# Moving one tap of a short convolution to ScalarE and GpSimd, and the z gate's two scalings to other steps

## The chip, the cores and the metric

One NeuronCore of a Trainium2 chip runs the whole program. The metric is the time of one execution in microseconds (us) of device time. A profile is one execution taken by the hardware profiler. PE is TensorE (PEld its weight loads), DVE is VectorE, ACT is ScalarE, POOL is GpSimd, SP is the engine whose queue issues most DMAs.

## The reference, cut to what matters

A decoder trunk of two layers on 512 tokens with model width 1024, in float32. Each layer normalizes its input, projects it with one wide matrix, and feeds three mixers: A (a gated MLP over positions), B (attention with a window of 128) and C (a gated delta rule). Their results are projected, weighted by sigmoid gates, summed and added to the input; a SwiGLU block follows. The change touches mixer C alone, in two places.

```python
def causal_short_conv(x, w):              # x: q, k and v of mixer C, 1536 channels
    xp = jnp.pad(x, ((0, 0), (DN_CONV - 1, 0), (0, 0)))
    out = xp[:, 0:S_] * w[0]
    for i in range(1, DN_CONV):           # DN_CONV = 4 taps
        out = out + xp[:, i:i + S_] * w[i]
    return jax.nn.silu(out)
...
    o = rmsnorm(o, norm_g) * jax.nn.silu(z)   # o: 4 heads x 128; norm_g: 128 weights, one per head channel
```

So each of the 1536 channels gets a causal filter of four taps, and the result of the delta rule is normalized, weighted by `norm_g` and gated by z.

## The kernel before, in words

Every float32 product of the projections is made of three matmuls: a weight tile is split into a high part `wh` (ACT) and a low part `wl` (DVE), the activations likewise, and high by high, high by low and low by high are summed in one PSUM bank. A projection tile of 128 x 1024 weights is 24 matmuls of 512 columns. Tiles that the convolution needs come out with channels on partitions (`fm_tile`, line 343); those of z come out with tokens on partitions (`tm_group`, line 349), four banks at a time. Four PSUM banks (`mm`) serve these projections, four (`px`) everything small.

The first half of a layer is called the mixing part here. One dense stream runs the projections in the order k, z, q and v of heads 0 and 1, q and v of heads 2 and 3, aq, gv, u (`ORDER`, line 44), and then the gates. Beside it run small streams: `decay` (line 583), `keys` (602), `queries` (640), `values` (665) and `scan` (678) of the delta rule, `blocks` (824) and `solves` (747) for its triangular systems, attention and the position mixing. `keys` sends a matrix to DRAM by a DMA on POOL's queue (`blkscr`), `blocks` fetches it back (`nx`), inverts 16 x 16 blocks on DVE and passes the result through DRAM again (`cols`), and `solves` begins with the products of `Tc`. The gates may not begin before the last step of `scan`, so what the dense stream has left by then (above all `u`, four tiles) is what PE has to fill the waits of the small streams with.

The order of PE's instructions is fixed when the program is built. A planner (`Issue`, lines 51 to 161) walks through all streams with costs of its own: an elementwise step on DVE or ACT counts 0.07 us plus columns / 960, a two-input step on POOL 0.1 us plus columns / 430, each with a latency `LAT` of 0.7 us on top. A small stream goes on at the time that the planner gives for its inputs; until then the dense stream fills in. Only PE's order is written out; the other engines' instructions are put in order by the framework, each engine's in one queue, and each engine works through its queue in order.

The convolution of one tile of 128 channels (`dn_conv`, line 530) takes the projection out of its bank with a scaling (`pre`, DVE), multiplies by the last tap on ACT (`cv`), adds the three other taps with one DVE instruction each, makes the SiLU with a tanh on ACT and a last DVE instruction that writes `dk`, `dq` or `dv`. `rot` buffers (five of them, line 190) hold `pre` and `cv`. There are 12 tiles per layer, 24 in all.

The z gate (`z_proj`, line 1104) is made per 128 tokens: a tanh on ACT out of the bank, a DVE instruction that forms (tanh + 1) times the bank's value, and a second DVE instruction that scales by the token's norm (`rsth`) and by the weight `dn` (`norm_g`, loaded repeated over all partitions, 128 x 128). That is four groups per layer, eight in all. `scan` later multiplies this gate with its normalized result, in place (`zg`). `branch_c` (line 1059) turns the result with PE transposes and splits it into a high part (`bH`, ACT) and a low part (`bL`, DVE) for the branch's projection.

A constant `pad` of `PAD` columns (line 224) stands among the first tiles and takes up room only.

Of the kernel before, what the change touches and what calls it, by code (L numbers as in the profile page):

```python
# [10 lines left out]
F32 = mybir.dt.float32  # L11
F32R = mybir.dt.float32r
I32 = mybir.dt.int32
AF = mybir.ActivationFunctionType
ALU = mybir.AluOpType
# [3 lines left out]
P = 128  # L19
T = 512  # L20
# [17 lines left out]
LAT = 0.7  # L38
DMA_LAT = 2.5
DENSE = 10  # L40
PAD = 112
SOON = 200
ORDER = "k z qv0 qv1 aq gv u"

# [120 lines left out]
def hybrid_kernel(ctx, tc, x0, pos, wi, wkv, wb, wo, wg, wd, gn, convw, lngb, sguw, sgub,  # L165
                  sinks, alog, dtb, dnn, wt, gf, out, depth=DEPTH):
    issue = Issue()
    nc = issue.front(tc.nc)
# [11 lines left out]
    def nm(s):  # L180
        uid[0] += 1
        return f"{s}_{uid[0]}"
# [7 lines left out]
    def rot(name):  # L190
        return base.tile([P, T], F32, tag="rot", name=nm(name), bufs=N_ROT)
# [7 lines left out]
    def cst(shape, name, dt=F32):  # L199
        return const.tile(shape, dt, name=name, tag=name)  # L200
# [22 lines left out]
    gnt = cst([P, 2 * DEPTH, KT], "gnt")  # L223
    cst([P, PAD], "pad")
    nc.sync.dma_start(gnt, gn)
# [207 lines left out]
    def layer(l, norm, first=None):  # L433
# [6 lines left out]
        def lp(shape, name, src, pool=lay):  # L440
            t = pool.tile(shape, F32, tag=name, name=nm(name))
            nc.sync.dma_start(t, src)
            return t

        cw = lp([P, 12, 4], "cw", convw[l])
        snk = lp([P, 8], "snk", sinks[l])
        al = lp([P, 4], "al", alog[l])
        db = lp([P, 4], "db", dtb[l])
        dn = lp([P, P], "dn", dnn[l])
        lnc = lp([P, 8], "lnc", lngb[l])  # L450
        nsnk = lay.tile([P, 8], F32, tag="nsnk", name=nm("nsnk"))
        nc.vector.tensor_scalar(nsnk, snk, -1.0, None, ALU.mult)
# [1 line left out]
        def br_tiles(th, tl):  # L454
            return ([pg(th, "brH", dt=F32R) for i in range(4)], [pg(tl, "brL", dt=F32R) for i in range(4)])
# [5 lines left out]
        banks = yield from tm_group(first or [wkv[l, j] for j in range(4)], 264, xs, ("mm", "px", "px", "px"))  # L461
        vt = pg("kv", "vt", [P, NCH, P])
        rst8 = lay.tile([P, NCH], F32, tag="rst8", name=nm("rst8"))
        rsth = lay.tile([P, NCH], F32, tag="rsth", name=nm("rsth"))
# [65 lines left out]
        def dn_conv(ti, dst, ps):  # L530

            yield f"rep{norm.gi}"
            pre = rot("pre")
            nc.vector.tensor_tensor(pre, ps, norm.rep, ALU.mult)
            cv = rot("cv")
            nc.scalar.activation(cv, pre, AF.Copy, scale=cw[:, ti, 3:4])
            for i in (2, 1, 0):
                n = 3 - i
                nc.vector.scalar_tensor_tensor(cv[:, n:], pre[:, :T - n], cw[:, ti, i:i + 1], cv[:, n:],
                                               ALU.mult, ALU.add)  # L540
            nc.scalar.activation(pre, cv, AF.Tanh, scale=0.5)
            nc.vector.scalar_tensor_tensor(dst, pre, 1.0, cv, ALU.add, ALU.mult)
# [14 lines left out]
        def hs(hl):  # L557
            return slice(hl * P, (hl + 1) * P)
# [500 lines left out]
        def branch_c():  # L1059

            for e in (f"gA{l}", f"A{l}", f"o{l}0{NCH - 1}", f"o{l}1{NCH - 1}"):
                yield e
            bH, bL = br["C"] = br_tiles("fm", "kd")
            for i in range(4):
                pt = bank("px")
                for c in range(NCH):
                    nc.tensor.transpose(pt[:, hs(c)], zg[c][:, hs(i)], ident)
                nc.scalar.copy(bH[i], pt)
                nc.vector.tensor_tensor(bL[i], pt, bH[i].bitcast(F32), ALU.subtract)
                yield  # L1070
            issue.set(f"C{l}")

# [31 lines left out]
        def z_proj():  # L1104
            banks = yield from tm_group([wi[l, CI_Z + j] for j in range(4)], 512, xs)
            yield f"gg{l}"
            for c in range(NCH):
                z = zg[c]
                nc.scalar.activation(z, banks[c], AF.Tanh, scale=rsth[:, c:c + 1])
                nc.vector.scalar_tensor_tensor(z, z, 1.0, banks[c], ALU.add, ALU.mult)  # L1110
                zv = z.rearrange("p (h e) -> p h e", h=4)
                nc.vector.scalar_tensor_tensor(zv, zv, rsth[:, c:c + 1], dn.unsqueeze(1).broadcast_to([P, 4, P]),
                                               ALU.mult, ALU.mult)
            issue.set(f"z{l}")

        def keys_done():
# [17 lines left out]
        zg = [pg("zg", "zg", [P, T]) for c in range(NCH)]  # L1134
# [76 lines left out]
        with tc.tile_pool(name=f"ffn{l}", bufs=1, reuse_waits="tile") as fp:  # L1211
# [25 lines left out]
            for m in range(KT):  # L1237
                pd = mm_bank()
                for j, (k0, k1) in enumerate(((0, 8), (8, 16), (16, 22))):
                    w = wload(wd[l, m, :, k0 * P:k1 * P], (k1 - k0) * P)  # L1240
# [108 lines left out]
def _rep(a):  # L1349
    return np.ascontiguousarray(np.broadcast_to(a[..., None, :], a.shape[:-1] + (P,) + a.shape[-1:]))  # L1350


def _layout(x, positions, attn_norm, w_in, sgu_ln_g, sgu_ln_b, sgu_w, sgu_b, attn_sinks, dn_conv_w, dn_a_log,
            dn_dt_bias, dn_norm, w_branch, w_out, ffn_norm, w_gate_up, w_down, final_norm):
    L = w_in.shape[0]
    cuts = np.cumsum([0, 512, 512, 512, 128, 128, 1536, 512, 4, 4, 3072])
    perm = np.concatenate([np.arange(h * 64, (h + 1) * 64) for h in HEAD_PERM])
    wi, wkv, wb, wg, wd, wo = [], [], [], [], [], []
    for l in range(L):
        u, v, q, k, vb, qkv, z, be, a, gt = [w_in[l][:, cuts[i]:cuts[i + 1]] for i in range(10)]  # L1360
        wi.append(np.concatenate([_tiles_fm(qkv), _tiles_fm(u), _tiles_tm(q[:, perm]), _tiles_tm(v), _tiles_tm(z),
                                  _tiles_fm(gt)]))
        wkv.append(_tiles_tm(np.concatenate([k, vb, be, a], axis=1)))
        br = []
        for i in range(3):
            w = w_branch[l, i][perm] if i == 1 else w_branch[l, i]
            t = _tiles_fm(w)
            br.append(t.reshape(4, 2, P, 512).transpose(0, 2, 1, 3).reshape(4, P, 1024))
        wb.append(np.stack(br))
        wo.append(_tiles_fm(w_out[l]))  # L1370
        g = _tiles_fm(w_gate_up[l])
        wg.append(np.stack([g[:KF], g[KF:]], axis=1).reshape(2 * KF, P, 1024))
        if l < L - 1:
            wd.append(_tiles_fm(w_down[l]))
    gn = np.stack([attn_norm, ffn_norm], axis=1).reshape(2 * L, D)
    return {
        "x0": x[0].T.reshape(KT, P, T),
        "pos": positions[0].reshape(NCH, P).T,
        "wi": np.stack(wi), "wkv": np.stack(wkv), "wb": np.stack(wb), "wo": np.stack(wo), "wg": np.stack(wg),
        "wd": np.stack(wd),  # L1380
        "gn": gn.reshape(2 * L, KT, P).transpose(2, 0, 1),
        "convw": dn_conv_w.reshape(L, 4, 12, P).transpose(0, 3, 2, 1),
        "lngb": np.concatenate([sgu_ln_g, sgu_ln_b], axis=1).reshape(L, 8, P).transpose(0, 2, 1),
        "sguw": sgu_w.transpose(0, 3, 1, 2),
        "sgub": _rep(sgu_b.reshape(L, 512)).reshape(L, P, 4, P),
        "sinks": _rep(attn_sinks[:, HEAD_PERM]),
        "wt": w_down[L - 1].reshape(KF, P, D), "gf": _rep(final_norm),
        "alog": _rep(dn_a_log), "dtb": _rep(dn_dt_bias), "dnn": _rep(dn_norm),
    }


# [21 lines left out]
```

## Time and profile before

| what | value |
|---|---|
| three runs | 1724.6, 1725.21 (median), 1727.14 us |
| the profiled execution's own time | 1728.58 us |
| its span, first to last instruction | 1726.5 us |
| PE busy | 1706.7 us (99%) |
| DVE busy | 852.8 us (49%) |
| ACT busy | 648.0 us (38%) |
| POOL busy | 414.8 us (24%) |

The profiled execution took 3.37 us more than the median of the runs, and 2.08 us of its time lie outside the span. Matmuls overlap one another and their ends are modelled, so PE's busy share says where PE had work, not how fast it went; the waits in front of PE's instructions are what tells of lost time. The two mixing parts lie at about 9 to 315 us and 862 to 1172 us of the span; between and after them run the dense SwiGLU blocks.

### The profile page before, as it was taken

How to read it: one execution, taken by the hardware profiler on the slowest of the kernel's cores; microseconds unless marked ns; L12 is line 12 of the kernel's file. 1: busy time of each engine (PE TensorE's matmuls, PEld its weight loads, DVE VectorE, ACT ScalarE, POOL GpSimd, SP SyncE). 2: the span in 40 equal slices, each digit the busy share in tenths (PEclk: the TensorE clock that was granted, in tenths of full speed). 3: DMA queues.
4: the chain of work that ended last, by engine and by line, in shares of the span. 5: the costliest groups of instructions: out<-in, count | busy, mean ns of one | idle time of the engine just before them, and what ended most of it. 6: DMA issues, size and time to landing. Idle time of an engine off the chain costs nothing.

```text
span 1726.5 us, 22439 instructions
## 1 busy us (share of the span) xinstructions
PE 1706.7 (99%) x8580; PEld 1410.4 (82%) x8580; DVE 852.8 (49%) x1624; ACT 648.0 (38%) x1206; POOL 414.8 (24%) x457
## 2 busy tenths in 40 slices
PE   9999999999999999999999999999999999999998
PEld 8888778888888888888888877788888888888886
DVE  7685874544543333323276948644444433333224
ACT  6454663323342222222245546532233322222212
POOL 3423231021223333310024133210212233333000
PEclk9999999999999999999999999999999999999999
DMA  5232112232443223344332220122224534444332
GB/s 163 93 104 90 38 46 96 86 98 90 130 153 99 97 97 98 98 128 125 109 117 98 95 80 26 57 91 91 98 98 134 164 105 120 120 122 158 98 98 85
DMA packets 73116, 176.59 MB, mean 102 GB/s; under 512 B 24945, under 2 KB 25201, under 8 KB 73009
## 3 DMA queue, kind: packets, MB, share of 16 engines
q1 hardware_dynamic: 71184, 170.71, 31.0%
q0 software_dynamic: 1248, 3.41, 0.7%
q8 instruction: 67, 1.10, 0.3%
q10 hardware_dynamic: 576, 1.05, 0.2%
q14 instruction: 41, 0.33, 0.1%
HBM read 162.03 MB, written 13.11 MB: 101 GB/s over the span
## 4 chain that ended last, share of the span: by engine, by line
PE 95%; DVE 2%; ACT 1%; POOL 1%; issue 0%; DMA 0%; SPq 0%; POOLq 0%; ACTq 0%; DVEq 0%
PE mm L120 83%; PE px L120 12%; DVE U L120 0%; DVE wl L120 0%; DMA x<-in_x 0%; ACT pr L120 0%; POOL of L120 0%; DVE xf L120 0%; DVE pr L120 0%; DVE S L120 0%; DVE zg L120 0%; DVE Tc L120 0%; ACT wh L120 0%; POOL pr L120 0%; ACT ojk L120 0%
## 5 line engine op out<-in xcount | busy, mean ns | idle before, releaser
L120 ACT CAST wh<-st 128x1024 fp32r<-128x1024 f32 (+2 forms) x286 | 295.6, 1033 | 815.5 <-PE mm L120 611.0
L120 PE MATMUL mm<-hH,wh 128*128 128x512 f32 x1344 | 532.9, 396 | 0.0
L120 PE MATMUL mm<-hH,wl 128*128 128x512 f32 x1344 | 524.7, 390 | 0.0
L120 PE MATMUL mm<-hL,wh 128*128 128x512 f32 x1344 | 524.1, 390 | 0.0
L120 DVE TENSOR_TENSOR wl<-st,wh 128x1024 fp32r<-128x1024 f32 (+2 forms) x286 | 353.5, 1236 | 226.8 <-ACT wh L120 216.6
L120 PEld LDWEIGHTS mm<-hH,wh 128*128 128x128 f32 x1344 | 253.1, 188 | 53.2 <-issue 2.7
L120 PEld LDWEIGHTS mm<-hH,wl 128*128 128x128 f32 x1344 | 252.8, 188 | 53.3
L120 PEld LDWEIGHTS mm<-hL,wh 128*128 128x128 f32 x1344 | 253.2, 188 | 51.2 <-issue 1.2
L120 POOL TENSOR_TENSOR s<-s,rep 128x512 f32<-128x512 f32 x44 | 77.5, 1762 | 162.1 <-ACT s L120 162.1
L120 POOL TENSOR_TENSOR aL<-s,aH 128x512 fp32r<-128x512 f32 x44 | 77.6, 1764 | 156.3 <-ACT aH L120 152.6
L120 POOL TENSOR_TENSOR gt<-gt,gt 128x512 f32<-128x512 f32 x32 | 48.8, 1524 | 267.8 <-DVE gt L120 267.8
L120 DVE TENSOR_TENSOR s<-mm,s 128x512 f32<-128x512 f32 x44 | 30.4, 692 | 143.6 <-PE mm L120 136.8
L120 DVE TENSOR_TENSOR s<-mm,rep 128x512 f32<-128x512 f32 x44 | 30.4, 692 | 138.2 <-PE mm L120 111.2
L120 DVE TENSOR_TENSOR gt<-mm,rep 128x512 f32<-128x512 f32 x48 | 33.1, 690 | 107.5 <-PE mm L120 107.5
L120 PE MATMUL mm<-wh,hH 128*128 128x512 f32 (+1 forms) x208 | 83.2, 400 | 0.8 <-ACT hH L120 0.8
L120 PE MATMUL mm<-wh,hL 128*128 128x512 f32 (+1 forms) x208 | 79.9, 384 | 0.7 <-DVE hL L120 0.7
L120 PE MATMUL mm<-wl,hH 128*128 128x512 f32 (+1 forms) x208 | 79.5, 382 | 0.0
L120 PE MATMUL mm<-brH,wh 128*128 128x512 f32 x192 | 74.7, 389 | 0.0
L120 PE MATMUL mm<-brL,wh 128*128 128x512 f32 x192 | 74.7, 389 | 0.0
L120 PE MATMUL mm<-brH,wl 128*128 128x512 f32 x192 | 74.7, 389 | 0.0
L120 PE MATMUL mm<-aH,wh 128*128 128x512 f32 x176 | 68.5, 389 | 0.0
L120 PE MATMUL mm<-aL,wh 128*128 128x512 f32 x176 | 68.5, 389 | 0.0
(290 smaller groups left out, 2446.2 us busy)
## 6 DMA issues: line engine op xcount, KB each, us to landing
st<-in_wi SPq DMA_DIRECT2D x104, 512.0 KB, 3.3
st<-in_wg SPq DMA_DIRECT2D x88, 512.0 KB, 3.4
st<-in_wb SPq DMA_DIRECT2D x24, 512.0 KB, 3.4
st<-in_wt SPq DMA_DIRECT2D x22, 512.0 KB, 3.3
st<-in_wo SPq DMA_DIRECT2D x16, 512.0 KB, 3.6
st<-in_wd SPq DMA_DIRECT2D x16, 512.0 KB, 3.5
xscr<-xt SPq DMA_DIRECT2D x24, 256.0 KB, 2.0
xt<-xscr SPq DMA_DIRECT2D x24, 256.0 KB, 2.8
```

Source lines behind the costliest of these rows:

```text
L120: return f(*args, **kw)
```

## The change

- The tap that reaches back three tokens is no longer added by DVE. ACT multiplies `pre` by it, into the tile that will hold the convolution's result (`dst`), and POOL adds that to `cv`. DVE then adds the two other taps. DVE's next step thus waits for POOL.
- z is scaled by the token's norm as ACT takes it out of the bank; a tanh from SBUF into a `rot` buffer follows, and one DVE instruction instead of two. The bank is read by ACT alone.
- The weight `norm_g` is loaded as one column (128 x 1) and applied in `branch_c`, where channels are on partitions: as the scale of ACT's step and as the scalar of DVE's.
- `PAD` goes from 112 to 231 columns.

```diff
-PAD = 112
+PAD = 231
...
-        dn = lp([P, P], "dn", dnn[l])
+        dn = lp([P, 1], "dn", dnn[l])
...
             cv = rot("cv")
             nc.scalar.activation(cv, pre, AF.Copy, scale=cw[:, ti, 3:4])
-            for i in (2, 1, 0):
+            nc.scalar.activation(dst[:, 3:], pre[:, :T - 3], AF.Copy, scale=cw[:, ti, 0:1])
+            nc.gpsimd.tensor_tensor(cv[:, 3:], cv[:, 3:], dst[:, 3:], ALU.add)
+            for i in (2, 1):
                 n = 3 - i
                 nc.vector.scalar_tensor_tensor(cv[:, n:], pre[:, :T - n], cw[:, ti, i:i + 1], cv[:, n:],
                                                ALU.mult, ALU.add)
...
-                nc.scalar.copy(bH[i], pt)
-                nc.vector.tensor_tensor(bL[i], pt, bH[i].bitcast(F32), ALU.subtract)
+                nc.scalar.activation(bH[i], pt, AF.Copy, scale=dn)
+                nc.vector.scalar_tensor_tensor(bL[i], pt, dn, bH[i].bitcast(F32), ALU.mult, ALU.subtract)
...
-                z = zg[c]
-                nc.scalar.activation(z, banks[c], AF.Tanh, scale=rsth[:, c:c + 1])
-                nc.vector.scalar_tensor_tensor(z, z, 1.0, banks[c], ALU.add, ALU.mult)
-                zv = z.rearrange("p (h e) -> p h e", h=4)
-                nc.vector.scalar_tensor_tensor(zv, zv, rsth[:, c:c + 1], dn.unsqueeze(1).broadcast_to([P, 4, P]),
-                                               ALU.mult, ALU.mult)
+                z, w = zg[c], rot("zt")
+                nc.scalar.activation(z, banks[c], AF.Copy, scale=rsth[:, c:c + 1])
+                nc.scalar.activation(w, z, AF.Tanh)
+                nc.vector.scalar_tensor_tensor(z, w, 1.0, z, ALU.add, ALU.mult)
...
-        "alog": _rep(dn_a_log), "dtb": _rep(dn_dt_bias), "dnn": _rep(dn_norm),
+        "alog": _rep(dn_a_log), "dtb": _rep(dn_dt_bias), "dnn": dn_norm.reshape(L, P, 1),
```

## Rows read from the trace of the kernel before

**Rows 1.** The page: busy time of each engine; the last chain's shares by engine.
```profile
PE 1706.7 (99%) x8580; PEld 1410.4 (82%) x8580; DVE 852.8 (49%) x1624; ACT 648.0 (38%) x1206; POOL 414.8 (24%) x457
...
PE 95%; DVE 2%; ACT 1%; POOL 1%; issue 0%; DMA 0%; SPq 0%; POOLq 0%; ACTq 0%; DVEq 0%
```

**Rows 2.** Busy time by stretch: length, then each engine, granted clock, DMA share, GB/s.
```profile
36.00:175.00 139.00, 137.95 (x800) 114.77 (x800) 96.78 (x235) 70.95 (x186) 49.00 (x80) 1.00 0.29 93
175.00:260.00 85.00, 82.74 (x643) 64.62 (x638) 67.49 (x236) 54.60 (x160) 28.09 (x45) 0.98 0.14 47
883.00:1013.00 130.00, 130.00 (x650) 108.73 (x649) 90.18 (x197) 65.41 (x160) 40.77 (x64) 1.00 0.31 99
1013.00:1116.00 103.00, 96.30 (x806) 74.55 (x806) 75.09 (x275) 60.41 (x183) 28.49 (x49) 0.98 0.14 45
1070.10:1073.60 3.50, 3.50 (x12) 2.31 (x11) 2.58 (x19) 2.63 (x12) 1.92 (x5) 0.51 0.00 0
```

**Rows 3.** Waits of PE: us in total, times, longest us.
```profile
PE px L120 <- DVE U L120: 2.5, 1, 2.5
PE px L120 <- ACT pT L120: 1.9, 2, 1.2
PE px L120 <- POOL pr L120: 1.5, 3, 0.6
...
PE px L120 <- POOL lg L120: 0.3, 1, 0.3
```

**Rows 4.** Groups of instructions, DVE: busy us, mean ns, idle before them.
```profile
L120 DVE SCALAR_TENSOR_TENSOR cv<-pre,cw,cv 128x511 f32<-128x511 f32 (+2 forms) x72 | 53.2, 747 | 1.6 <-ACT cv L120 1.0
L120 DVE SCALAR_TENSOR_TENSOR zg<-zg,rsth,dn 128x512 f32<-128x512 f32 x8 | 6.5, 809 | 0.2
```

**Rows 5.** Groups of instructions, ACT.
```profile
L120 ACT ACTIVATE cv<-pre,cw 128x512 f32<-128x512 f32 x24 | 17.2, 722 | 9.5 <-DVE pre L120 7.6 <-DVE dk L120 1.9
L120 ACT ACTIVATE pre<-cv 128x512 f32<-128x512 f32 x24 | 15.1, 631 | 32.6 <-DVE cv L120 32.5
L120 ACT ACTIVATE zg<-mm,rsth 128x512 f32<-128x512 f32 x8 | 5.5, 688 | 3.7 <-PE mm L120 3.7
L120 ACT CAST brH<-px 128x512 fp32r<-128x512 f32 x8 | 4.7, 585 | 11.6 <-PE px L120 11.6
```

**Rows 6.** Four tiles' instructions: duration ns min/median/max, first and last start, forms.
```profile
L120 POOL TENSOR_TENSOR gt<-gt,gt x32: 1282/1290/2332, 352.4 to 1315.7; 128x512 f32<-128x512 f32 x32
...
L120 POOL TENSOR_TENSOR nk<-ss,half x16: 707/928/1316, 77.7 to 962.2; 128x2 f32<-128x2 f32 x16
...
L120 POOL TENSOR_SCALAR lg<-tri_gt,gg x32: 362/372/1340, 35.0 to 917.2; 128x128 f32<-128x128 f32 x32
...
L120 DVE SCALAR_TENSOR_TENSOR cv<-pre,cw,cv x72: 739/748/753, 39.1 to 982.2; 128x511 f32<-128x511 f32 x24, 128x510 f32<-128x510 f32 x24, 128x509 f32<-128x509 f32 x24
```

**Rows 7.** Timeline, layer 0: start us, us; z's first weight tile split, z's first matmul.
```profile
34.84 1.23 DVE L120 TENSOR_TENSOR wl<-st,wh 128x1024 fp32r<-128x1024 f32 x1
...
44.72 0.39 PE L120 MATMUL mm<-wh,hH 128*128 128x512 f32 x1
```

**Rows 8.** Timeline, layer 0: the last two key convolutions, the first use of keys.
```profile
53.34 1.29 DVE L120 SCALAR_TENSOR_TENSOR dk<-pre,cv 128x512 f32<-128x512 f32 x2
...
75.75 0.38 PE L120 MATMUL px<-ident,dk 128*128 128x128 f32 x2
```

**Rows 9.** Timeline, layer 1: the last value convolution, transposes of values after it.
```profile
983.82 0.68 DVE L120 SCALAR_TENSOR_TENSOR dv<-pre,cv 128x512 f32<-128x512 f32 x1
...
988.89 0.38 PE L120 MATMUL px<-ident,dv 128*128 128x128 f32 x2
```

**Rows 10.** Timeline, both layers: first tiles of the solves written, first use.
```profile
147.97 0.90 DVE L120 TENSOR_TENSOR Tc<-cols,blk 128x128 f32<-128x128 f32 x4 [6.43 <-DMA cols<-sc]
...
162.61 1.09 PE L120 MATMUL px<-Tc,la 64*64 64x64 f32 x30
...
997.66 0.90 DVE L120 TENSOR_TENSOR Tc<-cols,blk 128x128 f32<-128x128 f32 x4 [4.98 <-DMA cols<-sc]
...
1013.61 1.15 PE L120 MATMUL px<-Tc,la 64*64 64x64 f32 x32
```

**Rows 11.** Timeline, layer 0, around z: POOL's decay inputs, PE's wait for them.
```profile
69.71 2.91 POOL L120 TENSOR_SCALAR lg<-tri_gt,gg 128x128 f32<-128x128 f32 x4 [2.57 <-PE px L120]
...
71.99 1.18 PE L120 MATMUL px<-tri_le,lg 128*128 128x128 f32 x6 [0.33 <-POOL lg L120]
```

## The prediction

> **What bounds the kernel now.** I read the page first: PE is busy 99% of the span and the chain of work that ended last lies 95% on PE, so an edit on another engine counts only where PE waits for it [rows 1]. Then the busy time by stretch. The convolutions lie in 36 to 175 us and 883 to 1013 us; there PE is idle for 139.00 - 137.95 = 1.05 us in layer 0 and not at all in layer 1, although DVE is busy 70% and 69% of the time. PE's idle time lies behind them, where the scans, solves and attention run: 85.00 - 82.74 = 2.26 us in layer 0 and 103.00 - 96.30 = 6.70 us in layer 1 [rows 2]. Then PE's waits: the longest are for U of the scan, for attention's pT and for its probabilities pr, none of which the change touches; one, 0.3 us for lg, stands beside z [rows 3, 11]. Last come the groups and tiles for the prices, and the timeline for the slack between a result and its first use on PE.
>
> **The change part by part.**
>
> *The tap.* DVE loses 24 of the 72 instructions of cv, 24 x 0.747 = 17.9 us, 9 us per layer [rows 4]. ACT gains 24 like its cv, 24 x 0.722 = 17.3 us [rows 5]; in the two stretches ACT goes from 51% and 50% to about 57%. POOL gains 24 additions of 509 columns. The trace has POOL's two-input step at 512 columns, gt: 1.282 at least, 1.290 in the middle, 2.332 at most [rows 6]. I take 1.29, as most of these are there: 31 us, with 56 us at the upper end; POOL is busy 35% and 31% of the two stretches [rows 2], so it has the room.
>
> DVE's next tap now waits for POOL, which waits for ACT. Per convolution that is longer by 0.722 (the second ACT step stands behind the first) + 1.29 - 0.747 = 1.3 us, between 1.26 and 2.3 us by the ends of gt. Queued behind the waiting DVE step are the bank's next eviction, the small steps of keys and the splits wl. PE waits for none of them at such a size: z's first weight tile is split at 36.07 and needed at 44.72, 8.6 us later [rows 7]; the last keys are done at 54.63 and needed at 75.75, 21 us later [rows 8]; the tightest result, the last dv of layer 1, is done at 984.50 and its earliest possible use is at 988.89, 4.4 us later [rows 9]. So 2.3 us more is hidden everywhere, and so is DVE's gain: 0. Without that cover each of 24 convolutions would cost up to 2.3 us.
>
> On POOL the additions stand in front of nk and of the blkscr DMA of keys, and with these in front of blocks and solves. An addition ahead of each of the four steps of a layer's keys would delay the solves by 4 x 1.29 = 5.2 us, 9.3 us at the upper end. The first Tc is complete at 148.87 and needed at 162.61, 13.7 us later; in layer 1 it is 998.56 and 1013.61, 15.0 us [rows 10]. Hidden too: 0.
>
> The row that shows the two engines in each other's way is nk, 0.707 us at least and 1.316 at most, and lg, 0.362 and 1.340, with cv never over 0.753 [rows 6]. The Trainium skill (SBUF — State Buffer, Who interferes with whom) states it as a lock: of a GpSimd step and a VectorE step with two SBUF inputs the one that issues second waits for the whole of the other. By that rule an addition could also hold back DVE's small steps of keys for its full 1.29 us, at four steps 5.2 us more in front of the solves; that stays inside the slack and the sum, but the late chain among the rivals would deserve 0.1 and not the 0.04 that I give it by the rows, where only POOL has waited beside cv.
>
> *The z gate.* DVE loses eight instructions of 0.809, 6.5 us [rows 4]. ACT's eight evictions stay at 0.688 and eight tanh from SBUF come on top, 8 x 0.631 = 5.0 us, as the convolution's tanh shows [rows 5]. The bank is free one DVE step earlier. That matters for nothing that PE waits for, but the removed DVE steps ran beside lg: the four lg at 69.71 took 2.91 us where 4 x 0.372 = 1.5 is usual, and PE waited 0.33 us behind them [rows 6, 11]. I book the 0.33 us as gained: -0.3; the other end is a wait that stays or doubles, +0.3, since a tanh on ACT now stands before la of the same stream. The rot buffers that z takes were last used by the keys' convolutions, done 15 us before this place [rows 8, 11].
>
> *The weight in branch_c.* ACT's eight steps go from 0.585 to at most the 0.722 of a scaled copy, 1.1 us in all [rows 5], DVE's stay. The result is used by the third branch, after two other branches and its own gates. 0; bounds 0 and +1.1.
>
> *dn and PAD.* 64 KB less per layer on a queue whose loads PE doesn't wait for after its start: 0. The pad grows by 476 bytes and dn shrinks by 508, so that what lies behind both keeps its place to within 32 bytes. 0.
>
> *PE's order.* This is the part that I can't read from a row. The planner prices the removed DVE tap at 0.07 + 509/960 + 0.7 = 1.30 us and the addition at 0.1 + 509/430 + 0.7 = 1.98 us, so keys, queries and values become ready 0.7 us later for it, about a step of three matmuls, while its DVE queue is shorter by 0.6 us per convolution, which acts the other way on the small steps. Some px groups will trade places with dense triples in both layers, and the waits behind 175 and 1013 us will be dealt anew. The same code has been dealt twice already: 2.26 us idle in layer 0, 6.70 in layer 1. Each also holds one stretch at half clock: in layer 1, behind a PE that had just stood idle for 2.5 us [rows 3], the granted clock read 0.51, the lower of its two levels (1.2 instead of 2.4 GHz), for 3.5 us [rows 2], which costs 1.7 us; in layer 0 the mean of 0.98 over 85 us says the same. Bounds: if all of it went, -(2.26 + 6.70 + 2 x 1.7) = -12.4 us; if both layers came out like layer 1 with a second half-clock stretch each, +4.4 + 2 x 1.7 = +7.8 us. I take 0, because the two layers' mean is what a new deal gives.
>
> Sum: -0.3 us. Against the profiled execution's own 1728.58 us that is 1728.3; this execution lay 3.37 us above the median of the runs, 1725.21, and from there I get 1724.9 us.
>
> **The rivals.**
>
> *Faster: the new order is kinder to layer 1.* DVE's shorter queue lets the planner place the small steps earlier, more of the scan runs beside dense work, and layer 1's idle 6.70 us comes down to layer 0's 2.26, with its half-clock stretch gone: -4.4 - 1.7 = -6.1, 1719 us. For it: the waits there end in a chain of small steps [rows 3]. Against it: DVE's load behind 1013 us is the same as before, 73% [rows 2], and 15 us of slack lie between the convolutions and that stretch [rows 10].
>
> *Slower: the dense filler is spent before the scans are done.* The place is the last scan step, which the gates must await; the filler is u, four tiles of 24 matmuls. With keys 0.7 us later in the plan at each of four steps, u is handed out earlier relative to the scans, and from the point where it is spent PE stands idle for each us that the scan still takes. Layer 0 then becomes like layer 1, +4.4, with one more half-clock stretch, +1.7: 1731 us. For it: that already happens in layer 1. Against it: the DVE relief in the planner pulls the other way.
>
> *The chain to the solves really gets late.* If the additions waited for ACT in front of nk at every step as well (0.722 each) and were held by DVE to the upper end, the delay is 4 x (2.332 + 0.722) = 12.2 us, still under 13.7; it needs more than that, and then costs a us per us, some 3 us per layer: 1731 us.
>
> *The relief isn't one:* DVE's freed time is spent waiting for POOL. The time is then the forecast's.
>
> **How the numbers follow.** The forecast, with the last rival, 0.46; faster by the order 0.28; slower by the order 0.22; the late chain 0.04. About 0.2%, 3.5 us, is what a measurement of this kernel can tell from no change. The forecast's own range is 1721.8 to 1728.6. The faster case, around 1719, reaches down to 1716 for most of its chance, the slower ones, around 1731, up to 1733; with 1717 to 1732.5 about two in ten are left out. Of the forecast's 0.46 I count 0.02 to either side of its range; so faster 0.30, no change 0.42, slower 0.28.
>
> **What would show it.** Right: cv on DVE 48 times at 0.75, POOL's new additions near 1.3 us, ACT's second step near 0.72; PE still 99% busy; hardly any wait of PE for dk, dq, dv, wl or wh between 36 and 150 us and 883 and 1005 us; the wait for lg gone; the difference between the two spans made up of idle PE and half-clock stretches behind 175 and 1013 us. Wrong: PE waiting in the convolutions' stretch, a wait for Tc at the first solve, taps on DVE lengthened to a us or more that PE then waits for, or matmuls that take other than 0.39 us in the dense parts.

## The result: 1.6% slower, and the profile after

| | before | after |
|---|---|---|
| median | 1724.99 us (1724.6 to 1727.14) | 1752.70 us (1751.22 to 1754.73) |
| ratio | | 1.0159, 95% interval 1.0147 to 1.0172 |
| profiled execution | 1728.58 us, span 1726.5 | 1751.22 us, span 1749.5 |

The change costs 27.7 us. The forecast was 1724.9 us, with a range that ended at 1732.5; it was wrong. The page of the kernel after, busy time by engine and the chain of work that ended last:

```profile
PE 1709.2 (98%) x8580; PEld 1410.8 (81%) x8580; DVE 839.7 (48%) x1592; ACT 667.8 (38%) x1238; POOL 435.5 (25%) x481
...
PE 38%; DVE 3%; ACT 1%; DMA 0%; POOL 0%; issue 0%; POOLq 0%; ACTq 0%; DVEq 0%
```

The two profiled spans differ by 23.0 us, less than the medians, because the profiled execution lay 3.4 us above its median before and 1.5 us below it after. PE's idle time accounts for 20.5 of the 23.0 (from 1726.5 - 1706.7 = 19.8 [rows 1] to 1749.5 - 1709.2 = 40.3) and PE's busy time for 2.5. The same stretches of the kernel after (length, then busy time of PE, its loads, DVE, ACT, POOL, granted clock, DMA share, GB/s), moved along with the work where it had slipped:

```profile
36.00:175.00 139.00, 126.33 (x611) 104.44 (x610) 82.34 (x180) 72.93 (x174) 54.34 (x80) 0.95 0.26 85
175.00:283.00 108.00, 103.45 (x856) 82.48 (x856) 78.29 (x284) 63.44 (x187) 29.45 (x56) 1.00 0.16 52
896.00:1030.00 134.00, 128.53 (x636) 106.23 (x635) 85.04 (x182) 72.87 (x175) 56.88 (x77) 1.00 0.29 92
1030.00:1140.00 110.00, 101.29 (x833) 78.72 (x832) 76.42 (x278) 62.12 (x186) 26.57 (x49) 1.00 0.14 46
```

Against [rows 2] the convolutions' own stretches, which had 1.05 and 0 us of idle PE, now have 12.7 and 5.5; in the first the granted clock is 0.95, since it also holds two drops to half speed (at 50 and 156 us of the span). Behind the convolutions the idle time is 4.6 and 8.7 us where it was 2.3 and 6.7, in stretches that are longer by 23 and 7 us. PE's waits in the kernel after (us in total, times, longest):

```profile
PE px L120 <- DVE la L120: 10.1, 5, 6.3
PE mm L120 <- DVE pre L120: 6.0, 3, 3.2
PE px L120 <- DVE U L120: 2.5, 1, 2.5
PE px L120 <- ACT pT L120: 2.5, 3, 1.1
```

U and pT are the old ones [rows 3]. The first two are new, and neither is a wait for data: `pre` empties an `mm` bank, the last readers of the `px` banks are the DVE steps that write `la`. PE waits for a free bank. The tile cv of the kernel after (duration in ns: least, median, most), and one of the lines that say what its engine waited for, in us and times:

```profile
L120 DVE SCALAR_TENSOR_TENSOR cv<-pre,cw,cv x48: 730/750/1749, 39.3 to 1003.7; 128x511 f32<-128x511 f32 x24, 128x510 f32<-128x510 f32 x24
...
L120 POOL TENSOR_TENSOR cv<-cv,dk x8: 1269/1303/1749, 38.0 to 918.0; 128x509 f32<-128x509 f32 x8
...
L120 POOL TENSOR_TENSOR cv<-cv,dq x8: 1264/1274/1302, 81.2 to 985.8; 128x509 f32<-128x509 f32 x8
...
L120 POOL TENSOR_TENSOR cv<-cv,dv x8: 1263/1281/1303, 95.6 to 1000.9; 128x509 f32<-128x509 f32 x8
...
  POOL cv L120: 27.5, 17
```

The addition takes what was forecast. But DVE stood idle 27.5 us in front of its taps for POOL, 17 times, and seven of its steps that ran beside an addition were longer than usual by 6.5 us together: 34 us of DVE's time for the 17.9 us of taps that it was relieved of [rows 4]. The 34 us are an upper bound of what it lost, since a queue that isn't always full stands idle somewhere anyway: where DVE adds itself (e18 below), it still waits 4.9 us at this place for ACT's product. Where this reaches PE is seen at 50 us of the span. Timelines (start us, length, instruction, in brackets the idle time before it and its releaser); the last line is the same place in e18, with the same order of PE and no addition on POOL:

```profile
48.93 0.75 DVE L120 SCALAR_TENSOR_TENSOR cv<-pre,cw,cv 128x511 f32<-128x511 f32 x1 [1.15 <-POOL cv L120]
49.60 0.17 DVE L120 TENSOR_SCALAR negc<-ex 128x16 f32<-128x16 f32 x1
49.68 0.68 DVE L120 TENSOR_TENSOR pre<-mm,rep 128x512 f32<-128x512 f32 x1
...
47.15 1.75 POOL L120 TENSOR_TENSOR cv<-cv,dk 128x509 f32<-128x509 f32 x1 [5.93 <-ACT cv L120]
...
50.42 0.76 PE L120 MATMUL mm<-wh,hH 128*128 128x512 f32 x1 [3.18 <-DVE pre L120]
...
48.01 0.51 PE L120 MATMUL mm<-wh,hH 128*128 128x512 f32 x1 [1.06 <-DVE pre L120]
```

A tap stands at the head of DVE's queue until POOL's addition is done at 48.90; behind it stands the eviction `pre`, whose bank PE has wanted since 47.24. PE waits 3.18 us for it, and 1.06 in e18. PE's longest wait is another matter (the kernel after again):

```profile
150.24 0.61 DVE L120 SCALAR_TENSOR_TENSOR la<-px,sj,la 128x128 f32<-128x128 f32 x2
157.07 0.49 DVE L120 TENSOR_TENSOR Tc<-cols,blk 128x128 f32<-128x128 f32 x2 [6.22 <-DMA cols<-sc]
157.48 1.22 DVE L120 TENSOR_TENSOR wl<-st,wh 128x1024 fp32r<-128x1024 f32 x1
158.62 1.00 DVE L120 TENSOR_TENSOR Tc<-cols,blk 128x128 f32<-128x128 f32 x2
159.54 0.41 DVE L120 TENSOR_SCALAR ssq<-ssq 128x2 f32<-128x2 f32 x1
159.87 0.60 DVE L120 SCALAR_TENSOR_TENSOR la<-px,sj,la 128x128 f32<-128x128 f32 x2
```

```profile
153.87 0.38 PE L120 MATMUL px<-ident,dv 128*128 128x128 f32 x2
160.52 0.69 PE L120 MATMUL px<-ident,dv 128*128 128x128 f32 x2 [6.26 <-DVE la L120]
```

The blocks' chain is late (its nx transfer was issued at 131.49 where it was at 118.20). DVE waits 6.2 us at the head of its queue for `cols`; behind that stands the last `la`, whose bank PE wants at 154.25. PE doesn't need Tc there, yet it waits for the engine that waits for Tc's input. Most of this wait is the order's and not POOL's: in e18 it is 4.2 us and with the instructions of before (e4) 5.3, while in the kernel before DVE waits 6.43 us for `cols` too [rows 10] and PE, in its old order, wants no bank then.

### The profile page after: what moved, and what is told of

Read it like the earlier page. It is cut to its first block, busy times and chain, and to the rows that moved or that the text cites. A ratio compares the mean times of both kernels' runs of the same rounds, so it can differ in the third digit from the quotient of the medians.

```text
span 1749.5 us, 22456 instructions
## 1 busy us (share of the span) xinstructions
PE 1709.2 (98%) x8580; PEld 1410.8 (81%) x8580; DVE 839.7 (48%) x1592; ACT 667.8 (38%) x1238; POOL 435.5 (25%) x481
## 3 DMA queue, kind: packets, MB, share of 16 engines
q10 hardware_dynamic: 576, 1.05, 0.2%
```

## The experiments

The kernel before was run beside each of these; its medians lay between 1724.3 and 1725.1 us. In the diffs `tc.nc` issues an instruction of which the planner is not told, and `issue.note` tells the planner of one that is not issued: so instructions and PE's order can be set apart. "Order of before" means that PE's instructions stand in exactly that order.

### Which part, and is it PE's order or the instructions?

**e1_tap_only**: the diff's convolution alone, planned anew. **e2_z_only**: all of the diff but the convolution, planned anew.

> The convolution's part alone: the z gate, the weight dn and the pad are as before, the planner prices what it sees. If the tap's new wait (DVE behind POOL) or its new price in the plan makes the 27.7 us, this kernel is nearly as slow as the changed one: 1745 to 1757 us, PE waiting for pre and la in the convolutions' stretches. If the z gate with its rot buffers makes it, this kernel stays at 1722 to 1730 us.

> The z gate, dn, the weight in branch_c and the pad alone: the convolution is as before. If the tap makes the loss: 1720 to 1730 us. If the z gate does: over 1745 us. In between, the two add up, or the new deal of PE's order that each brings costs something by itself.

e1 1739.8 us, ratio 1.0083 [1.0067, 1.0099]; e2 1721.0 us, 0.9975 [0.9966, 0.9985]. The tap alone loses 15.3 us and the z part alone gains 3.4. Together that is 11.9 us and not 27.7, so the two parts don't simply add; what is missing shows up in the order next.

**e3_old_plan**: every instruction of the kernel after, the order of before. **e4_new_plan**: every instruction of before, the order of after. **e8_tap_plan**: every instruction of before, the order of e1.

```diff
 # e3
-            nc.gpsimd.tensor_tensor(cv[:, 3:], cv[:, 3:], dst[:, 3:], ALU.add)
+            real.gpsimd.tensor_tensor(cv[:, 3:], cv[:, 3:], dst[:, 3:], ALU.add)    # real = tc.nc
...
+            issue.note("vector", "scalar_tensor_tensor", (cv[:, 3:], pre[:, :T - 3], cv[:, 3:]), {})
```

> All instructions of the changed kernel, but the planner is told the prices of the kernel before, so that PE's instructions stand in the order of before, one for one. Theory 1 (execution): DVE's and ACT's queues stand behind the addition on POOL, so PE waits for its banks whatever its order: 1742 to 1765 us, possibly worse than the changed kernel because that order expects the results earlier. Theory 2 (order): the changed order is what costs, so this one is back at 1722 to 1730 us.

> All instructions of the kernel before, but the planner is told the prices of the changed one, so that PE's instructions stand in the order of the changed kernel, one for one. Theory 1 (execution): 1722 to 1732 us. Theory 2 (order): 1745 to 1757 us. If both this one and the kernel with the old order are slow in part, the two shares are read from the pair.

> All instructions of the kernel before, but the planner is told the price of the changed tap, not that of the changed z gate. PE's order is that of the kernel with the tap alone (1739.8 us). If POOL's price for the addition makes the bad order: about as slow as with both prices (1737.4 us), 1733 to 1742 us, and the instructions' share in the kernel with the tap alone is what is left. If it is the two prices together, or how an order happens to fall out: 1722 to 1730 us.

e3 1745.1, 1.0112 [1.0097, 1.0127]; e4 1737.4, 1.0069 [1.0052, 1.0085]; e8 1720.95, 0.9981 [0.9972, 0.9991]. Instructions and order both cost. The same instructions of before ran between 3.8 us faster and 13.0 us slower by the order alone. The tap's price by itself makes a good order (e8, -3.8), and with e3's +19.1 over e5 (below) that is the +15.3 of e1; only the two prices together make the bad one (e4).

**e18_after_dve_adds**: the kernel after with its own order, but DVE adds the product instead of POOL.

```diff
-            nc.gpsimd.tensor_tensor(cv[:, 3:], cv[:, 3:], dst[:, 3:], ALU.add)
+            tc.nc.vector.tensor_tensor(cv[:, 3:], cv[:, 3:], dst[:, 3:], ALU.add)
+            issue.note("gpsimd", "tensor_tensor", (cv[:, 3:], cv[:, 3:], dst[:, 3:]), {})
```

> The changed kernel in PE's own new order, with one thing undone: DVE adds the product instead of POOL (a plain addition of 0.69 us, 24 times); ACT's product, the z gate and branch_c stay as changed. (1) If the loss of 27.7 us is the sum of an order that is dearer with any instructions (e4, before's instructions in this order: 1737.4) and of POOL's additions: 1735 to 1739, so that POOL's additions are 14 to 18 us at this order too. (2) If the new order is dear only for instructions other than its own, so that e4 tells nothing of the changed kernel: 1727 or less. (3) If ACT's product and the z gate carry a share at this order: 1741 or more.

1735.8 us, 1.0061 [1.0045, 1.0078]. So 11.1 us are the order (with ACT's product and the z part, which cost nothing that is clear of noise in the order of before, e5 below), and 16.9 are POOL's additions. That the two make up the whole follows from the subtraction; what bears them out is that both came out alike elsewhere, 13.0 for the order with before's instructions (e4) and 19.1 for the additions in the order of before (e3 against e5). In the traces, too, the additions are nearly accounted for: against e18 PE's waits in the kernel after are longer by 4.7 us for `pre`, 4.5 for `la` and 1.9 for `dq`, and the granted clock is at half (1.2 instead of 2.4 GHz) for 13.6 us and not 6.8, leaving out the span's last 5 us, which is worth 3.4: 14.5 of the 14.9 us between the two spans. About half of the order's part is in PE's waits for `la` (of e18):

```profile
PE px L120 <- DVE la L120: 5.6, 2, 4.2
```

The longest ends at 150.5 us, in front of the transposes of dv, the place shown above: this order wants a bank there that DVE frees only behind its step for `cols`.

### What about POOL's addition costs?

**e5_dve_adds**: e3, but DVE adds the product. **e6_add_last**: e3, but POOL adds behind DVE's two taps, which so don't wait for it. **e7_pre_first**: e3 with `pre` at high priority, so that the evictions stand further ahead in DVE's queue.

> The kernel with all changed instructions and the old order of PE (1745.1 us), with one edit: ACT still makes the tap's product, but DVE adds it and POOL has no part in the convolution. Theory 1a (DVE's queue stands behind POOL's addition): the 20.7 us over before are gone, 1721 to 1730 us. Theory 1b (ACT's 24 further products and the tanh behind them hold up the weight splits or the keys): still 1735 us or more.

> As the kernel with the old order (1745.1 us), with one edit: POOL adds the product after DVE's two taps and not before them, so no tap waits for POOL; ACT's tanh does. The path through one convolution is as long as there. Theory 1a (the taps at the head of DVE's queue wait for POOL and hold up what is behind them): 1724 to 1735 us. If only the length of the path counted: 1742 to 1748 us.

> As the kernel with the old order (1745.1 us), with one edit: the eviction pre is given a high priority, so that it stands ahead of the waiting taps in DVE's queue (the fourth eviction of the keys does; in that kernel it stands behind two taps of the third). PE's wait for pre, 9.6 us there, should go, and with the half-clock stretch behind it the time should come to 1731 to 1737 us if bank evictions behind waiting taps are the half of it; if it stays at 1742 us or more, the evictions are late for another reason.

e5 1726.05, 1.0006 [0.9997, 1.0016]: ACT's product, the z part and branch_c cost nothing that is clear of noise, and POOL's addition makes the 19.1 us between e5 and e3. e6 1742.9, 1.0107 [1.0092, 1.0122]: the taps no longer wait, but DVE's last step of each convolution then waits for the tanh behind POOL, 19.8 us in 11 times (3.8 in e5). So e6 moved DVE's wait and did not take it away. e7 1747.1, 1.0132 [1.0117, 1.0147]: PE's wait for `pre` fell from 9.6 to 2.1 us and that for `la` rose from 1.6 to 6.7. The place of one step in the queue only moves the wait.

**e11_act_hop**: e5, with a copy on ACT in the path (the path is as long as with POOL). **e10_pool_beside**: e5, with an addition on POOL whose result nobody reads (one tanh waits 1.9 us until it has read `pre`). **e12_keys_only**: e3 with POOL's addition in the keys' 8 convolutions only.

```diff
 # e11, behind DVE's addition of e5
+            real.scalar.copy(cv[:, 3:], cv[:, 3:])
 # e10, at the same place
+            real.gpsimd.tensor_tensor(pad[:, 3:], pre[:, 3:], dst[:, 3:], ALU.add)
```

> As e5 (DVE adds the product, PE's order that of before, POOL has nothing new), but after the addition ACT copies cv in place, 509 columns, before DVE adds the two other taps. The result is the same. That puts about 0.65 us and two changes of engine on each convolution's path without POOL; POOL's addition in e3 put 1.29 - 0.75 = 0.54 us and two changes of engine there. (1) The path theory: a loss of the size of e3's, 1737 to 1750, with PE waiting for pre and la. (2) The POOL theory (what costs is POOL: its queue, or its place beside DVE): 1726 to 1730, the 24 x 0.65 = 15.6 us more on ACT being hidden.

> DVE adds the product, as in e5 (1726.0 us), and PE's order is that of before; but POOL gets an addition of the same size at the same place, of pre and the product into a constant tile that nobody reads. It waits for ACT's product as the real one does and stands in POOL's queue in front of nk and the blkscr and nx DMAs; DVE's taps don't wait for it. (1) The path theory (the loss of e3, 1745.1, comes because DVE's taps, and with them the bank evictions and la behind them in its queue, wait for POOL's result): 1725 to 1729. (2) The queue theory (POOL's own queue is held up, so nk, blkscr and nx come late): a third to all of e3's loss, 1732 to 1745, with the first nx DMA of layer 0 several us behind 114.9. (3) The neighbour theory (an addition on POOL holds DVE's steps of two SBUF inputs): the median of cv on DVE goes from 0.75 to over 0.9 us, and 1730 to 1740.

> e3 (PE's order that of before) with POOL's addition in the four key convolutions of each layer alone; in those of q and v DVE adds the product as in e5. 8 of the 24 additions stay. (1) If the loss lies in the keys (their chain through nk, blkscr and nx to the blocks and solves starts late): 60% or more of the 19 us between e5 and e3 stay, 1737 to 1745. (2) If each convolution costs about alike: a third, 1732. (3) If it lies where the convolutions of q and v meet the blocks and la in DVE's queue, as the waits of PE at 126 to 140 us of e3 look: under a fifth, 1726 to 1730.

e11 1725.8, 1.0006 [0.9997, 1.0015]; e10 1743.0, 1.0103 [1.0087, 1.0118]; e12 1729.2, 1.0024 [1.0015, 1.0033]. From the end of ACT's product to the first tap it took 1.97 us in e3 and 2.09 in e11 (means of 24), and 1.37 in e5. The longer path by itself is free. That does not clear DVE's waiting, for DVE hardly waits in e11: in the 75 us of layer 0 shown below it is busy for 60.2 us there and for 53.8 in e3. What DVE's taps waited for in e3, then in e11 (us, times, longest):

```profile
DVE cv L120 <- POOL cv L539: 21.4, 14, 3.4
```

```profile
DVE cv L120 <- ACT cv L540: 3.3, 5, 0.7
```

An addition on POOL beside the path costs 17 us, although no tap waits for it. Of the signs that e10 was to show, the queue theory's came, with its range of times: the first nx transfer is issued at 126.2 us and not at e5's 114.95. The neighbour theory's did not, since cv's median stays at 0.749 us; the steps that are held show in single long ones. The late transfer doesn't go along with the loss, though: it is 3.4 to 4.1 us behind e5's in e15, e12 and e6, which cost 4.5, 3.2 and 16.8 us. The keys' third of the additions costs 3.2 of the 19 us, so most of the loss comes only with those of q and v, where the blocks run too; a kernel with these alone was not run. What POOL's addition does to DVE in e10, in two timelines:

```profile
106.58 0.69 DVE L539 TENSOR_TENSOR cv<-cv,dv 128x509 f32<-128x509 f32 x1
107.19 1.25 DVE L120 TENSOR_TENSOR kds<-sj,ex 128x2 f32<-128x2 f32 x1
108.36 0.59 DVE L120 SCALAR_TENSOR_TENSOR la<-px,sj,la 128x128 f32<-128x128 f32 x2
...
106.22 0.71 POOL L120 TENSOR_TENSOR nk<-ss,half 128x2 f32<-128x2 f32 x1 [4.41 <-DVE ss L120]
106.91 1.50 POOL L540 TENSOR_TENSOR pad<-pre,dv 128x509 f32<-128x509 f32 x1
```

`kds`, two columns, ends with POOL's addition and takes 1.25 us; in e5 it took 0.15 to 0.16. Twenty-three DVE steps beside the 24 additions were lengthened so, by 23.3 us together (each against the usual length of its like).

**e14_dve_filler**: e5 with one more DVE instruction per convolution; **e17_two_fillers**: with two. **e15_pool_one_input**: e10 with a POOL step of one input; **e16_both**: e14 and e15 together.

```diff
 # e14, behind DVE's addition of e5; pad has 640 columns
+            real.vector.tensor_tensor(pad.rearrange("p (h e) -> p h e", h=5), pre[:, :P].unsqueeze(1).broadcast_to([P, 5, P]),
+                                      dst[:, 3:3 + P].unsqueeze(1).broadcast_to([P, 5, P]), ALU.add)
 # e15, at the same place
+            real.gpsimd.tensor_scalar(pad[:, 3:], dst[:, 3:], cw[:, ti, 0:1], None, ALU.mult)
```

> e5 (1726.0 us; DVE adds the product, PE's order that of before) with one more DVE instruction in each convolution, behind that addition: 640 columns, a sum of pre and the product into a constant tile that nobody reads, an estimated 0.95 us from wl's 1.23 us at 1024 columns and cv's 0.75 at 511. POOL has nothing new. In e10 DVE's steps were lengthened by 23.3 us beside POOL's 24 additions, 0.97 us each; in e3 DVE was lengthened by 8.6 us and stood idle 21 us in front of the taps. (1) If what the addition costs is time of DVE's queue (held or idle, it comes to the same): 24 x 0.95 = 23 us of DVE's time cost as much as in e3 and e10, 1738 to 1746. (2) If it is POOL's queue (nk, blkscr and nx standing behind the additions): 1726 to 1730. (3) Both in part: between.

> e10 (1743.0 us) with another step on POOL: instead of the addition of two tiles a multiplication of one tile, the product, by a column of weights, 509 columns, into the same tile that nobody reads. It waits for ACT's product and stands in POOL's queue in front of nk, blkscr and nx just as the addition did; estimated at 1.1 to 1.4 us from lg's 0.37 us at 128 columns. DVE's steps beside POOL's one-input steps lg and pr were hardly held (1 of 9 and 4 of 86 in e3). (1) If the loss is DVE's time, held by POOL's two-input addition: DVE's steps stay at their lengths, 1726 to 1730. (2) If it is POOL's queue: 1738 to 1745 as in e10. (3) If any POOL step of this size holds DVE: DVE's steps beside it are lengthened by a us, and 1738 to 1745; the two would then have to be told apart by e14.

> e14 and e15 in one kernel, the order of before: DVE's filler (0.82 us in each convolution, 19.7 us in all; alone 1730.6 us, 4.6 above e5) and POOL's one-input step (1.93 us each, DVE held by 6.2 us in all; alone 1730.6 us, 4.6 above e5), nobody waits for either. (1) If the two cost apart, each from slack of its own: 1726.0 + 4.6 + 4.6 = 1735, within 2 us. (2) If they draw on one slack, DVE's and POOL's queues taking turns at the small streams (DVE's ss for POOL's nk, DVE's la for POOL's blkscr), so that what one loses comes on top of what the other lost: more than the sum, 1739 to 1746, the size of e10 (1743.0), where POOL's step is shorter and DVE's loss 23.3 us. (3) If one hides behind the other: 1731 to 1733.

> e14 with DVE's filler twice in each convolution, 39.4 us of DVE's time instead of 19.7; POOL untouched, PE's order that of before. (1) If DVE's time costs in proportion (4.6 us for 19.7): 1735. (2) If there is a slack that the first filler has nearly used up, the second costs much more than the first: 1740 to 1750; then DVE's time alone can make a loss of e3's size, but only with about twice the time that POOL's addition takes from it.

The filler of e14 and the POOL steps of e15 (tile pad of each; durations in ns):

```profile
L540 DVE TENSOR_TENSOR pad<-pre,dq x8: 811/818/820, 81.7 to 965.8; 128x640 f32<-128x640 f32 x8
```

```profile
L540 POOL TENSOR_SCALAR pad<-dq,cw x8: 1571/1914/2063, 79.6 to 970.6; 128x509 f32<-128x509 f32 x8
```

| kernel (all in the order of before) | added to DVE's time | added to POOL | median | over e5 |
|---|---|---|---|---|
| e11 | none | none | 1725.8 | -0.2 |
| e14 | 19.7 us of filler | none | 1730.6 | +4.6 |
| e17 | 39.5 us of filler | none | 1747.8 | +21.7 |
| e15 | 6.2 us of lengthened steps | 46 us | 1730.6 | +4.5 |
| e16 | 20.9 us of filler, 6.4 us of lengthened steps | 50 us | 1738.4 | +12.4 |
| e10 | 23.3 us of lengthened steps | 38 us | 1743.0 | +16.9 |
| e3 | 21.4 idle + 8.6 lengthened - 16.6 for the addition | 32 us | 1745.1 | +19.1 |

The closest pair is e10 and e15. POOL's step stands at the same place and is longer in e15, yet e15 costs 12.4 us less; what differs is that DVE's steps are held by 6.2 us and not by 23.3 (and e10's tanh that waits 1.9 us for POOL). So most of what e10 costs is DVE being held. Both sides of e14's and e15's question were wrong by themselves: DVE's filler alone, and a long step in POOL's queue with little holding, cost a quarter each of what e10 costs. But DVE's time is enough to make a loss of this size, if it is more: the first 19.7 us cost 4.6, the second 17.2. In e17 PE waits for DVE's dq:

```profile
PE px L120 <- DVE dq L120: 13.4, 2, 8.5
```

The slack that the first filler used up can be read in the trace of the kernel before. The last dq of layer 1 is written at 968.26, and the transposes that read it begin at 972.26 (DVE, then PE):

```profile
967.57 0.69 DVE L120 SCALAR_TENSOR_TENSOR dq<-pre,cv 128x512 f32<-128x512 f32 x1
...
972.26 0.38 PE L120 MATMUL px<-ident,dq 128*128 128x128 f32 x2
```

These 4.0 us are what is there (1.5 in e5). At this very place PE waits 2.0 us in e3, 3.5 in e14, 3.7 in e10, 6.2 in e16 and 8.5 in e17. So most of the first filler's 19.7 us of DVE's time fits into a slack, and the second filler's is paid almost in full. That POOL's part draws on the same slack is not shown: e16 costs 3.3 us more than e14 and e15 add up to (9.1), which is within what the intervals allow, and its 1738.4 lies between the 1735 within 2 of separate slacks and the 1739 to 1746 of a shared one. The 75 us of layer 0 in which q's and v's convolutions, the keys' small steps and the blocks meet show how little DVE had left (before, then e3; columns as in the stretches above):

```profile
75.00:150.00 75.00, 75.00 (x389) 62.88 (x388) 60.38 (x159) 43.14 (x127) 20.25 (x24) 1.00 0.29 94
```

```profile
75.00:150.00 75.00, 68.88 (x346) 57.30 (x344) 53.78 (x144) 40.72 (x115) 30.20 (x34) 0.95 0.28 90
```

Before, DVE is busy 81% here, and its queue is in order, so part of the rest is waiting that it can't use. In e3 it does less in the same time, and PE 6 us less.

What stays open: how e3's 19 us divide. By the table its DVE lost 13.4 us net, less than e14's, yet it cost four times as much; and e16, which takes more of DVE's time and of POOL's than e10, costs 4.6 us less. So the price is no function of these two sums alone. That waiting at the head of the queue is dearer than being busy, because POOL, DVE and ACT then wait for one another in turn, would fit e3, e6 and e7, but no run separates it.

### A version that beats both

**e13_z_tap_plan**: the diff without the convolution, in the order of e8.

> The convolution of before (three taps on DVE) with the changed z gate, dn and branch_c, and PE's order exactly that of e8 (1720.95 us, which had before's instructions throughout). (1) If the z part's instructions cost and gain nothing in themselves and e2's 3.5 us were all a matter of order: 1721, the same as e8 within 1.5 us. (2) If they gain e2's 3.5 us themselves: 1717 to 1718.5. Either way faster than before; if it is over 1723, the z part's instructions cost something at this order.

1720.7 us, 0.9974 [0.9963, 0.9984], 0.25 us from e8: the z part's instructions cost and gain nothing in this order. That its 3.4 us in e2 go with e2's order, which is another one, is then likely but not shown: before's instructions were not run in it. e13, e8 and e2 are equally fast, 4 us before the kernel before and 32 before the one after.

## Why the prediction was wrong

- **What bounds the kernel:** read rightly (PE, and an edit counts where PE waits), but I took the mean of 70% over 139 us as room on DVE [rows 2]. In 75 to 150 us it is 81%. The sign that I had named for being wrong, PE waiting in the convolutions' stretch, came: 12.7 and 5.5 us of idle PE.
- **The tap, instructions and path: right in the main.** 48 taps of 0.75 and additions of 1.27 to 1.30 by their medians, and a path that is longer by 1.2 us (from cv's start to the tanh's at the least 3.11 us before and 4.35 after). A path of that length is free where ACT makes it (e11, 4.37 at the least). The slacks of 8.6, 21 and 4.4 us [rows 7 to 9] held: in the kernel after PE waits for no `wl` and no dk, and for dv only 1.6 us in the scan, as it does in e18. But the last dv was not the tightest result. The last dq of layer 1 had 4.0 us, and PE waits 1.9 us for it in the kernel after.
- **The tap, "and so is DVE's gain: 0": the step that failed.** I booked the 17.9 us less of taps as a gain that merely leads to nothing, and the wait for POOL as hidden everywhere. DVE's queue lost up to 34 us to waiting and lengthened steps instead, 16 net in the kernel after, and its time was near its limit (e14, e17). I had named what stands behind the waiting tap, the bank's next eviction and the small steps, but looked for their results' first uses. What PE waited for was above all the banks that they free: 4.7 us more for `pre` and 4.5 more for `la` than in e18. The term was 0; it measured 16.9 us (the kernel after against e18). How much of it is waiting and how much held steps stays open.
- **Two engines in each other's way: mis-weighed.** I wrote that only POOL had waited beside cv [rows 6], and gave the lock 5.2 us on the keys alone. The trace of before had the answer one tile further. Eight DVE steps, all of them `wl`, were issued while a two-input addition gt ran on POOL, and all eight took 2.27 to 2.34 us and not 1.23. One of them (DVE, then POOL; the kernel before):

```profile
355.24 2.28 DVE L120 TENSOR_TENSOR wl<-st,wh 128x1024 fp32r<-128x1024 f32 x1 [0.17 <-ACT wh L120]
...
355.15 1.29 POOL L120 TENSOR_TENSOR gt<-gt,gt 128x512 f32<-128x512 f32 x1 [1.43 <-DVE gt L120]
```

  It starts 0.09 us behind POOL's step and is 1.05 us longer than usual; SwiGLU's stretch has room for that, the convolutions' hasn't. The Trainium skill (SBUF — State Buffer, Who interferes with whom) says just this, that a DVE instruction with two SBUF inputs and a GpSimd instruction that reads SBUF exclude each other and that the order of issue decides who waits; e10 agrees, with 23 steps lengthened by about 1 us. e15 does not: its GpSimd step reads SBUF too, but two `wl` and three `kds`, each with two SBUF inputs, were issued while it ran and kept their usual lengths. The Trainium skill (Perfetto Trace Analysis, Optimizing Scalar/DVE Operations) also warns that moving work between these two engines may not help; e5 against e3 agrees, with 19.1 us.
- **POOL's additions in front of the solves:** forecast 5.2 us, 9.3 at most. The nx transfer came 13.3 us later in layer 0, 9.4 of them against e18 and so with the additions, 3.9 with the order. PE did not wait for Tc at the first solve, so the 13.7 us of slack [rows 10] were the wrong measure: it waited for a bank behind DVE's step for `cols`.
- **The z gate, branch_c, dn and PAD: right**, 0 within a us in the order of e8 (e13); the wait for lg is gone.
- **PE's order: 0, bounds -12.4 and +7.8: the second failure.** It measured +11.1 (e18), and +13.0 with before's instructions (e4). The bounds came from the idle time that the trace had, behind the convolutions. The new order lost at a place that had no wait before, 4.2 us at 150 us of the span (e18), where 6.8 us at half the granted clock go with it.
- **The rivals:** "the relief isn't one" named what DVE does, waiting for POOL, but priced it at the forecast's time; the late chain had 4% and 1731 us. No case went beyond 1733.

## What to carry to other kernels

- Before work goes from VectorE to GpSimd, look in the trace at what any two-input GpSimd step of that size does to the VectorE steps beside it, on all tiles: the hold counts against the relief, and here each addition took up to 1.4 us of VectorE's time, waiting and holds together (34 us over 24), for a tap of 0.75.
- In an in-order queue a step that waits holds up all that stands behind it. The slack to check is that of whatever frees a bank or a buffer in that queue, in the busiest 75 us, not only from a result to its first use.
- Where a planner orders the instructions, a changed price reorders them, and that alone was worth -3.8 to +13.0 us here. Run old instructions in the new order and new ones in the old before anything is put down to the edit.

## What the runs showed of the hardware

- A two-column VectorE step (`kds`) took 1.25 us beside a two-input GpSimd step of 1.50 us, where it takes 0.16 alone, and ended 0.02 us behind it: the hold went by what was left of the other's step, not by its own size.
- A one-input GpSimd step (e15) lengthened the DVE steps beside it far less: 18 of 79, by 0.3 us each and 6.2 in all. It is the slower one itself, 1.56 us at least for 509 columns where the two-input addition takes 1.27 at best, and longer than the 1.1 to 1.4 that were estimated for it.
- ScalarE's additional copies in e11 (0.62 us, 24 times, each in the path) were free: 1725.8 us against e5's 1726.05.
